# Hybrid decoder step on one core: the order of work set by a clock that follows each tile's data, attention halves ordered by events, output projection in order 0, 4, 1, 5

## The chip, the cores and the metric

The kernel runs on one core of a Trainium2 chip. The metric is the device time of one execution in microseconds (us). Three runs of the kernel before are given; their median is its time.

## The reference

One inference step of a two-layer decoder, model width 1024, for a prompt of 512 tokens and for 8 samples of 8 new tokens each, so 576 columns with the same weights. All is float32. Cut to what matters:

```python
def layer(x, ...):                         # x: tokens x 1024
    proj = rmsnorm(x, norm1) @ w_in        # 2304 for q, k, v; 512 for u; 1024 + 1024 for the gates
    q, k, v, u, ga, gb = split(proj)
    q, k = rope(q), rope(k)                # 12 heads of 64: groups (window 128, dilation 1), (512, 4), (2048, 16)
    o_a = attention(q, k, v)               # per group; the groups mixed by softmax of their log-sums
    o_b = pool(u) @ pool_lin * pool_scale  # causal means over 2, 4, 8, 16 tokens, less the token
    x = x + (sigmoid(ga) * (o_a @ w_pa) + sigmoid(gb) * (o_b @ w_pb)) @ w_o
    return x + square(relu(rmsnorm(x, norm2) @ w_up)) @ w_down
```

The samples attend to caches of 128, 512 and 1024 tokens and to their own new tokens. Updated caches and pooling states are outputs as well.

## The kernel before, in words

A float32 matrix product is made of three products: each operand is split into a high and a low part (hi, lo), and hi x hi, hi x lo and lo x hi are added up in PSUM. Weights come in tiles of 128 x 1024 through SyncE's DMA queue into `raw` (two buffers); ScalarE copies the high part (`wh`), VectorE subtracts the low part (`wl`). `wnext` (L218) hands out the next split tile, starts the reads that follow, and settles the splits that are owed.

Each layer runs these stages in TensorE's order:
- Projections to q, k, v, in units d, a, b, e, c for half 0 of the heads and d, a, b, c for half 1 (`qkv`, L535). `unit_out` (L564) scales a unit's result into `nat`, rotates it (`rope`), transposes it (`trq`), and writes it out (`out_p<-nat`). For unit c it sends the values through DRAM and back into `vc`.
- Beside them attention runs as generators. `prompt(p)` (L634) makes for half p four sets of scores (`sp`), adds the mask (`P<-sp`), reduces maxima (`stt<-P`), exponentiates, brings the sums of the groups across partitions with small matmuls (`ex<-xt`), scales P (`P<-P,cc`), transposes it (`trx`) and multiplies by the values; it ends with the event ("O", p). `decode_q` (L767) rotates the samples' queries (`rope<-dn`), sends them through DRAM (`DQ`, `DR`) and reads them spread over partitions (`qb`). `decode(p)` (L820) multiplies cached keys (`kc`) by `qb` on GpSimd (`prod`), reduces on VectorE (`SC<-prod`), makes the softmax (`dsm`, `mb`, TensorE's `po<-const,dsm`), and multiplies by cached values (`pb`).
- Pooling: four projections to u (`u<-mm,rb`), `windows` (L991), `lin` (L1038).
- Gates of the pooling branch (`tb`, `mB`), gates of the attention branch (`m`), eight blocks each.
- Output projection (L1170): eight blocks f; each result is added into `xs[f]` (`xr<-xr,mm`), and `blocks(f)` (L1146) prepares the operands of the MLP from it: a block under 4 needs one scaling, one subtraction and one split, a block of 4 or above needs six VectorE operations (it combines x[f] with x[f - 4]). `square` adds the squares for the norm.
- MLP with a Strassen-like scheme on the first product: `first_pairs` (L1281), then `both(j)` (L1307), then the end.

The instructions of all engines are written out by one pass of Python; each engine runs its own in that order. The order of the work beside TensorE's main stream is set by a small clock `now` (L240). Every step of a matrix product calls `tick` (L252), which advances `now` by a constant (0.72, 1.28, 0.85 or 0.4 us); small matmuls call `spend` (L249). `tick` then gives each waiting generator (`side`) one step if its time has come or the event that it waits for is marked (`mark`); `until` ticks until an event is there. `after(*lanes)` (L294) makes a generator wait until the queue of an engine is empty by the model of `Lane` (L276), which knows per engine a fixed cost and a rate, but not what an operation's data wait for. DMAs cost the model nothing.

## Time and profile before

| | |
|---|---|
| three runs | 1778.17, 1773.99, 1765.66 us |
| their median | 1773.99 us |
| profiled execution | 1766.39 us |
| span of its trace | 1764.6 us |
| busy: TensorE, VectorE, ScalarE, GpSimd | 1643.5, 1186.3, 667.1, 432.1 us |
| mean granted clock of TensorE | 0.959 |

The span goes from the first instruction to the last of the profiled execution; what lies around it is 1.8 us. A clock of 1.00 is the upper of TensorE's two levels (2.4 GHz); a mean of 0.9 in a stretch says that for a part of it the lower (1.2 GHz) was granted. Busy time is shown for each engine by itself; an engine that is not busy may wait for another or have nothing to do.

### The profile page before, as it was taken

How to read it: one execution, taken by the hardware profiler on the slowest of the kernel's cores; microseconds unless marked ns; L12 is line 12 of the kernel's file. 1: busy time of each engine (PE TensorE's matmuls, PEld its weight loads, DVE VectorE, ACT ScalarE, POOL GpSimd, SP SyncE). 2: the span in 40 equal slices, each digit the busy share in tenths (PEclk: the TensorE clock that was granted, in tenths of full speed). 3: DMA queues.
4: the chain of work that ended last, by engine and by line, in shares of the span. 5: the costliest groups of instructions: out<-in, count | busy, mean ns of one | idle time of the engine just before them, and what ended most of it. 6: DMA issues, size and time to landing. Idle time of an engine off the chain costs nothing. (4 is left out here: it accounts for less than half of the span.)

```text
span 1764.6 us, 30680 instructions
## 1 busy us (share of the span) xinstructions
PE 1643.5 (93%) x12608; PEld 1594.6 (90%) x12608; DVE 1186.3 (67%) x1801; ACT 667.1 (38%) x1142; POOL 432.1 (24%) x461
## 2 busy tenths in 40 slices
PE   8978798999899999999898897989997999999995
PEld 7978788989899999999898886888997999999995
DVE  6498579735776766666626985893467766666763
ACT  4523332223454434344434342321344443344443
POOL 2074129211111111121103702562111111111202
PEclk9989899999899999999999998999998999999998
DMA  4551654434235554552427346525250544554511
GB/s 172 169 180 59 211 160 125 136 104 142 105 120 191 181 169 167 189 189 70 138 74 232 116 139 189 145 90 162 76 203 29 180 169 179 191 175 165 178 63 54
DMA packets 140006, 255.21 MB, mean 145 GB/s; under 512 B 9661, under 2 KB 100285, under 8 KB 137035
## 3 DMA queue, kind: packets, MB, share of 16 engines
q1 hardware_dynamic: 135498, 198.46, 35.0%
q0 software_dynamic: 3648, 53.98, 8.5%
q8 instruction: 99, 1.62, 0.4%
q10 hardware_dynamic: 720, 0.82, 0.1%
q14 instruction: 41, 0.33, 0.1%
HBM read 239.40 MB, written 74.87 MB: 178 GB/s over the span
## 5 line engine op out<-in xcount | busy, mean ns | idle before, releaser
L316 PE MATMUL mm<-m,wh 128*128 128x256 f32 (+1 forms) x2304 | 399.6, 295 | 2.0 <-DVE xr L291 1.1
L316 PEld LDWEIGHTS mm<-m,wh 128*128 128x128 f32 x2304 | 343.9, 188 | 2.9 <-issue 1.3
L291 DVE TENSOR_TENSOR wl<-raw,wh 128x1024 fp32r<-128x1024 f32 (+2 forms) x195 | 264.6, 1358 | 105.7 <-ACT wh L291 103.2
L291 POOL TENSOR_TENSOR prod<-kc,qb 128x1024 f32<-128x1024 f32 (+1 forms) x96 | 210.3, 2222 | 221.4 <-DMA kc<-in_c 178.1
L291 ACT CAST wh<-rawu 128x512 fp32r<-128x512 f32 (+1 forms) x158 | 123.1, 783 | 352.1 <-DVE rawu L291 301.4
L316 PE MATMUL mm<-m,wl 128*128 128x256 f32 (+1 forms) x1152 | 247.1, 296 | 1.8 <-DVE wl L291 1.8
L291 ACT CAST wh<-raw 128x1024 fp32r<-128x1024 f32 (+2 forms) x195 | 183.3, 940 | 170.8 <-PE mm L316 58.7
L316 PE MATMUL mm<-a,wh 128*128 128x256 f32 (+1 forms) x1280 | 235.4, 307 | 10.6 <-DVE mB L291 5.5
L546 PE MATMUL mmq<-wh,a 128*128 128x256 f32 x1152 | 225.9, 296 | 4.4 <-DVE a L291 2.5
L316 PEld LDWEIGHTS mm<-a,wh 128*128 128x128 f32 x1280 | 196.1, 195 | 18.7 <-issue 18.1
L546 PEld LDWEIGHTS mmq<-wh,a 128*128 128x128 f32 x1152 | 188.1, 200 | 8.0 <-DVE a L291 3.2
L316 PEld LDWEIGHTS mm<-m,wl 128*128 128x128 f32 x1152 | 193.0, 188 | 2.3 <-DVE wl L291 2.3
L291 POOL COPY pace<-beat 1x1 f32<-1x1 f32 x112 | 60.7, 542 | 540.3 <-DVE beat L291 540.3
L291 DVE TENSOR_TENSOR wl<-rawu,wh 128x512 fp32r<-128x512 f32 (+1 forms) x158 | 143.8, 911 | 63.1 <-ACT wh L291 60.5
L1217 PE MATMUL pa<-h,wh 128*128 128x288 f32 x896 | 181.6, 295 | 0.0
L291 DVE TENSOR_TENSOR xr<-xr,mm 128x576 f32<-128x576 f32 (+2 forms) x152 | 108.7, 716 | 106.5 <-PE mm L316 93.1
L546 PE MATMUL mmq<-wl,a 128*128 128x256 f32 x576 | 167.9, 292 | 0.0
L1217 PEld LDWEIGHTS pa<-h,wh 128*128 128x128 f32 x896 | 144.8, 188 | 0.0
L316 PE MATMUL mm<-a,wl 128*128 128x256 f32 (+1 forms) x640 | 139.4, 300 | 0.0
L1217 PE MATMUL pa<-h,wl 128*128 128x288 f32 x448 | 132.4, 296 | 0.0
L546 PEld LDWEIGHTS mmq<-wl,a 128*128 128x128 f32 x576 | 115.1, 200 | 0.0
L316 PEld LDWEIGHTS mm<-a,wl 128*128 128x128 f32 x640 | 110.4, 194 | 0.0
(226 smaller groups left out, 2744.1 us busy)
## 6 DMA issues: line engine op xcount, KB each, us to landing
out_s<-in_c POOLq DMA_DIRECT2D x64, 508.0 KB, 5.0
rawu<-in_wup SPq DMA_DIRECT2D x60, 512.0 KB
raw<-in_wd SPq DMA_DIRECT2D x60, 512.0 KB
kc<-in_c SPq DMA_DIRECT2D x40, 512.0 KB
raw<-in_wq SPq DMA_DIRECT2D x35, 512.0 KB
kc<-in_c SPq DMA_DIRECT2D x64, 256.0 KB
out_s<-in_c POOLq DMA_DIRECT2D x32, 504.0 KB, 5.3
raw<-in_wgb SPq DMA_DIRECT2D x16, 512.0 KB
```

Source lines behind the costliest of these rows:

```text
L291: return op(*args, **kw)
L316: T.matmul(ps[:, c0:c0 + t1 - t0], w, act[:, x, t0:t1], start=(i == 0 and j == 0), stop=(i == n - 1 and j == 2))
L546: T.matmul(psm[:, j], x, ww, start=(k == 0 and i == 0 and j % 2 == 0), stop=(k == 7 and i == 2 and j % 2 == 1), skip_group_check=True)
L1217: T.matmul(dst, w[m][:, c], ops[name][k][:, x], start=(start and k == 0 and j == 0), stop=(stop and k == 3 and j == 2), skip_group_check=True)
```

## The change

No operation is added to the device's work or taken from it, but for the order. Five things change.

1. The clock. `tick()` no longer advances time, and `spend` is gone. TensorE's engine is wrapped in a class `Matrix`, and `Lane` is rewritten: each operation starts, in the model, when its engine is free and when the data that it reads (and the buffers that it writes) are ready, tile by tile, region by region (`place`, `due`, `note`). DMAs are modelled by `transfer` (270 GB/s on one wire, 1.9 us to land). VectorE's two-input operations take longer in the model while GpSimd's lane is in use. `now` is TensorE's modelled time. `ready(*aps)` is a wait for given data.
2. Halves by events. `prompt(1)` waits for ("O", 0); so does the read of `vc` for half 1, which moved into a generator `turn`; the rotation of unit d of half 1 waits for ("S", 0), the event of half 0's scores.
3. The output projection takes its blocks in the order 0, 4, 1, 5, 2, 6, 3, 7, with the weights in that order too. The squares are numbered by position.
4. `stats` waits for the squares' sum before its matmuls, and its start after the output projection is 1.0 instead of 5.0 us of the clock.
5. `both(j)` waits for the norm's event ("R", ("b", l)).

The diff, cut:

```diff
+WO = (0, 4, 1, 5, 2, 6, 3, 7)
...
-        seq += [(a["wo"][l, f], 1024) for f in range(8)]
+        seq += [(a["wo"][l, f], 1024) for f in WO]
@@ -273 @@
+    def due(outs, ins, me):
+        t = 0.0
+        for x in ins:
+            key, a = place(x)
+            t = max([t] + hits(slots[key][1], a, me))
+        for x in outs:
+            key, a = place(x)
+            t = max([t, slots[key][0]] + hits(slots[key][1], a, me) + hits(slots[key][2], a, me))
+        return t
...
             def run(*args, **kw):
-                x = kw.get("in_", kw.get("out", args[0] if args else None))
-                n = 1
-                for d in x.shape[1:]:
-                    n *= d
-                self.t = max(self.t, now[0]) + self.fixed + n / self.rate
+                outs, ins = operands(args, kw)
+                if name == "dma_start":
+                    transfer(self, outs, ins)
+                    return op(*args, **kw)
+                t = max(self.t, due(outs, ins, self))
+                d = max(size(x) for x in outs + ins) / self.rate
+                if self is V and G.t > t and sum(x.space != PSUM and size(x) > 128 for x in ins) > 1:
+                    d = min(1.4 * d, 0.7 * d + G.t - t)
+                t += self.fixed + d
...
+                self.t = t
+                note(outs, ins, t, self)
                 return op(*args, **kw)
...
+    def transfer(lane, outs, ins):
+        lane.t = max(lane.t, due(outs, ins, None)) + (0.5 if lane is G else 0.06)
+        n = 4e-3 * outs[0].shape[0] * size(outs[0])
+        wire[0] = max(wire[0], lane.t) + n / 270.0
+        note(outs, ins, wire[0] + 1.9, wire)
+
+    class Matrix:
...
+        def go(self, out, ins, cost):
+            self.t = max(self.t, due([out], ins, self)) + cost
+            now[0] = max(now[0], self.t)
+            note([out], ins, self.t, self)
+
+        def matmul(self, out, w, x, **kw):
+            n = size(x)
+            self.go(out, (w, x), n * 0.458e-3 if x.dtype == F32R else max(0.2, n * 1.7e-3))
+            return self.eng.matmul(out, w, x, **kw)
...
-    V = Lane(V, 0.07, 960.0)
-    S = Lane(S, 0.19, 1400.0)
-    G = Lane(G, 0.1, 460.0)
+    T = Matrix(T)
+    V = Lane(V, 0.13, 960.0)
+    S = Lane(S, 0.19, 1190.0)
+    G = Lane(G, 0.12, 440.0)
+    Q = Lane(Q, 0.0, 1.0)
@@ gemm @@
-            tick(0.72)
+            tick()
@@ stats @@
+        yield ready(sqs)
@@ unit_out @@
-            if unit == "c":
-                DV = drp.tile([512, 256], F32, tag=f"dv{l}{p}", name="DV")
-                vc = pp.tile([128, 4, 256], F32, tag="vc", name="vc", bufs=1)
-                vcs[p] = vc
-                post(1.2, lambda: Q.dma_start(DV.rearrange("(j p) f -> p j f", j=4), nat))
-                post(4.0, lambda: Q.dma_start(vc, DV.rearrange("(n r) f -> n r f", r=4)))
-                mark("V", unit, p, lat=9.0)
...
+            if p and unit == "d":
+                yield ("S", 0)
+            if unit == "c":
+                side(turn(p, nat))
...
+        def turn(p, nat):
+            DV = drp.tile([512, 256], F32, tag=f"dv{l}{p}", name="DV")
+            Q.dma_start(DV.rearrange("(j p) f -> p j f", j=4), nat)
+            yield 2.8
+            if p:
+                yield ("O", 0)
+            vcs[p] = pp.tile([128, 4, 256], F32, tag="vc", name="vc", bufs=1)
+            Q.dma_start(vcs[p], DV.rearrange("(n r) f -> n r f", r=4))
+            mark("V", "c", p, lat=3.0)
+
         def prompt(p):
+            if p:
+                yield ("O", 0)
             yield ("T", "b", p)
@@ output projection @@
-        for f in range(8):
-            if f == 0:
+        for i, f in enumerate(WO):
+            if i == 0:
...
-            square(xs[f], sqs, f)
-        side(stats(sqs, False, ("b", l)), 5.0)
+            square(xs[f], sqs, i)
+        side(stats(sqs, False, ("b", l)), 1.0)
@@ both @@
+            until("R", ("b", l))
```

What this does to the order of instructions is shown at three places of layer 0. First, VectorE around the small product `ex` of half 0, in the second half of the projections (`xt` is its input, `SC<-prod` the reduces of decode's products). Before:

```order
L291 TENSOR_REDUCE stt<-P 128x2 x2
L291 TENSOR_TENSOR wl<-raw,wh 128x1024
L291 TENSOR_REDUCE SC<-prod 128x8x2
L291 TENSOR_TENSOR xt<-stt,const 128x16x2 x2
L291 TENSOR_REDUCE SC<-prod 128x8x2
L291 COPY ct<-ex 128x16
L291 TENSOR_TENSOR cc<-ct,stt 128x8
```

and now:

```order
L352 TENSOR_TENSOR wl<-raw,wh 128x1024
L352 SCALAR_TENSOR_TENSOR dn<-psd,rs,dt 64x128
L352 SCALAR_TENSOR_TENSOR ve_257<-psd,rs,dt 64x128
L352 TENSOR_REDUCE SC<-prod 128x8x2 x2
L352 TENSOR_TENSOR xt<-stt,const 128x16x2 x2
L352 TENSOR_REDUCE SC<-prod 128x4x2
L352 TENSOR_TENSOR wl<-raw,wh 128x1024
L352 TENSOR_REDUCE SC<-prod 128x4x2
L352 TENSOR_REDUCE SC<-prod 128x8x2 x2
L352 SCALAR_TENSOR_TENSOR dn<-psd,rs,dt 64x256
L352 TENSOR_TENSOR wl<-raw,wh 128x1024
L352 COPY ct<-ex 128x16
```

Two reduces stand ahead of `xt` instead of one. What follows `ct` (the sums, and behind them the scalings and transposes of P) stands later too, behind more of the reduces. The rotation of decode's queries (`rope<-dn`) stands one weight split later than before. On SyncE's queue the read `qb<-DR` now stands in front of a weight read (`raw<-in_wq`) that stood before it, and two reads of `kc` follow.

Second, TensorE where the projections end and the pooling projections (`mm<-a`) begin: the scores of half 1 (`sp`), set by set. Before (six matmuls `mm` are one step of the clock, eight steps one projection):

```order
L316 MATMUL mm<-a,wl 128x256
L316 MATMUL mm<-a,wl 128x320
L654 MATMUL sp<-Td 128x256 x2
L657 MATMUL sp<-Tb,Ta 128x128 x4
L316 MATMUL mm<-a,wh 128x256
L316 MATMUL mm<-a,wh 128x320
L316 MATMUL mm<-a,wh 128x256
L316 MATMUL mm<-a,wh 128x320
L316 MATMUL mm<-a,wl 128x256
L316 MATMUL mm<-a,wl 128x320
L883 MATMUL po<-const,mb 128x16
L316 MATMUL mm<-a,wh 128x256
```

and now:

```order
L375 MATMUL mm<-a,wl 128x256
L375 MATMUL mm<-a,wl 128x320
L375 MATMUL sp<-Td 128x256 x2
L375 MATMUL sp<-Tb,Ta 128x128 x4
L379 MATMUL po<-const,mb 128x16
L375 MATMUL sp<-Td 128x256 x2
L375 MATMUL sp<-Tb,Ta 128x128 x4
L375 MATMUL sp<-Td 128x256 x2
L375 MATMUL sp<-Tb,Ta 128x128 x4
L375 MATMUL po<-dsm,const 128x16
```

Before, the last two of the four sets stand apart by projections, and the first two stand in the last unit. Now all four stand behind that unit, three of them without a projection between.

Third, VectorE in the first gates, at the softmax of decode of half 1 (`dsm`; `mt` and `mb` follow TensorE's `po<-const,dsm`). Before:

```order
L291 TENSOR_TENSOR wl<-raw,wh 128x512
L291 TENSOR_TENSOR SC<-SC,const 128x368
L291 TENSOR_REDUCE dsm<-SC 128x16
L291 TENSOR_REDUCE mt<-po 16x8
L291 COPY mb<-mt 16x128
L291 TENSOR_TENSOR tb<-mm,rb 128x576
L291 TENSOR_TENSOR SC<-SC,po 128x368
L291 TENSOR_TENSOR wl<-raw,wh 128x1024
L291 TENSOR_REDUCE dsm<-SC 128x16
```

and now:

```order
L352 TENSOR_TENSOR wl<-raw,wh 128x512
L352 TENSOR_TENSOR SC<-SC,const 128x368
L352 TENSOR_REDUCE dsm<-SC 128x16
L352 SCALAR_TENSOR_TENSOR mB<-tb,mm 128x576
L352 TENSOR_TENSOR wl<-raw,wh 128x1024
L352 TENSOR_REDUCE mt<-po 16x8
L352 COPY mb<-mt 16x128
L352 TENSOR_TENSOR SC<-SC,po 128x368
L352 TENSOR_TENSOR tb<-mm,rb 128x576
L352 TENSOR_REDUCE dsm<-SC 128x16
```

The chain from `dsm` on stands earlier, and an `mB` and a whole weight split lie within it. On TensorE `po<-const,dsm` stands 102 matmuls (17 steps of six) earlier.

In the output projection VectorE's operations are the same, block by block, in the new order of blocks.

## Rows read from the trace of the kernel before

**Rows 1.** The page's first part: span, and busy time of each engine.
```profile
span 1764.6 us, 30680 instructions
...
PE 1643.5 (93%) x12608; PEld 1594.6 (90%) x12608; DVE 1186.3 (67%) x1801; ACT 667.1 (38%) x1142; POOL 432.1 (24%) x461
```

**Rows 2.** Busy time by stage, six of layer 0, two of layer 1.
```profile
core 0: us, PE busy (x) PEld busy (x) DVE busy (x) ACT busy (x) POOL busy (x), PEclk, DMA share, GB/s
84.15:183.03 98.88, 83.78 (x649) 79.56 (x647) 84.97 (x107) 31.23 (x59) 51.71 (x24) 0.90 0.45 135
183.03:212.72 29.69, 19.14 (x139) 17.52 (x139) 15.45 (x26) 11.24 (x37) 5.93 (x12) 0.84 0.81 261
248.00:332.70 84.70, 78.50 (x574) 76.49 (x572) 80.87 (x83) 22.54 (x37) 53.29 (x24) 0.98 0.36 106
332.70:372.00 39.30, 36.90 (x335) 32.20 (x334) 13.20 (x24) 6.72 (x11) 10.78 (x19) 0.91 0.58 170
372.00:429.00 57.00, 57.00 (x430) 57.00 (x428) 28.28 (x36) 19.52 (x28) 8.82 (x7) 1.00 0.29 91
429.00:506.00 77.00, 67.79 (x471) 66.97 (x470) 53.62 (x83) 37.59 (x62) 9.22 (x7) 0.89 0.36 120
950.10:1047.93 97.83, 82.97 (x649) 79.25 (x648) 84.73 (x107) 31.26 (x59) 50.74 (x24) 0.91 0.44 135
1112.00:1200.00 88.00, 79.51 (x580) 77.29 (x578) 77.76 (x86) 23.17 (x38) 54.55 (x24) 0.98 0.37 109
```

**Rows 3.** TensorE's timeline: start us, us, instruction, [idle before, what ended it].
```profile
94.02 1.22 PE L686 MATMUL ex<-xt,const 128*128 128x16 f32 x5 [3.95 <-DVE xt L291]
...
117.44 0.30 PE L733 MATMUL trx<-const,P 128*128 128x128 f32 x1 [1.85 <-DVE P L291]
...
156.41 0.88 PE L609 MATMUL trq<-const,nat 128*128 128x128 f32 x3 [4.01 <-DVE nat L291]
...
207.93 0.80 PE L905 MATMUL po<-pb,kvn 128*128 128x128 f32 x2 [9.11 <-POOL pb L291]
...
480.39 0.82 PE L1217 MATMUL mm<-h,wh 128*128 128x288 f32 x2 [6.18 <-DVE xr L291]
```

**Rows 4.** VectorE's operations by form, 84 to 160 us: count, busy, mean ns.
```profile
L291 DVE TENSOR_SCALAR P<-P,cc 128x256 f32<-128x256 f32 x14 | 17.3, 1277 | 0.0
L291 DVE TENSOR_TENSOR wl<-raw,wh 128x1024 fp32r<-128x1024 f32 x6 | 11.5, 1913 | 0.9 <-ACT wh L291 0.9
```

**Rows 5.** The same view, 208 to 248 us.
```profile
L291 DVE TENSOR_SCALAR P<-P,cc 128x256 f32<-128x256 f32 x14 | 4.3, 349 | 0.0
```

**Rows 6.** Timelines of GpSimd and VectorE at decode's first products.
```profile
87.87 9.60 POOL L291 TENSOR_TENSOR prod<-kc,qb 128x1024 f32<-128x1024 f32 x5 [70.88 <-DMA kc<-in_c]
...
90.34 1.22 DVE L291 TENSOR_REDUCE SC<-prod 128x16 f32<-128x1024 f32 x1 [3.55 <-POOL prod L291]
91.47 2.40 DVE L291 TENSOR_TENSOR xt<-stt,const 128x32 f32<-128x32 f32 x2
```

**Rows 7.** Timelines of VectorE and of SyncE's queue: the way of decode's queries.
```profile
63.46 0.61 DVE L291 TENSOR_TENSOR rope<-dn,const 64x192 f32<-64x192 f32 x2
...
66.71 1.23 DVE L291 TENSOR_TENSOR wl<-raw,wh 128x1024 fp32r<-128x1024 f32 x1 [2.18 <-ACT wh L291]
...
77.48 0.33 SPq L780 DMA_DIRECT2D qb<-DR  x1
```

**Rows 8.** VectorE's timeline, a set of scores and the first pooling projection.
```profile
191.91 1.29 DVE L291 TENSOR_TENSOR P<-sp,const 128x512 f32<-128x512 f32 x2 [0.30 <-PE sp L657]
193.11 1.27 DVE L291 TENSOR_REDUCE stt<-P 128x2 f32<-128x512 f32 x2
...
205.30 0.69 DVE L291 TENSOR_TENSOR u<-mm,rb 128x512 f32<-128x512 f32 x1 [10.22 <-DMA out_p<-nat]
```

**Rows 9.** VectorE's timeline: the adds of output blocks 6 and 7.
```profile
469.55 0.75 DVE L291 TENSOR_TENSOR xr<-xr,mm 128x576 f32<-128x576 f32 x1
...
479.49 0.75 DVE L291 TENSOR_TENSOR xr<-xr,mm 128x576 f32<-128x576 f32 x1
```

More of the change, by code (lines that the diff above doesn't have):

```diff
@@ L247, in mark @@
         ev[key] = now[0] + lat
-    def spend(us):
-        now[0] += us
     def tick(us=0.0):
@@ L274, in until, with place @@
             assert n < 2000, key
+    slots, seen, count = {}, {}, {}
+    def place(x):
+        t = x.tensor
+        key = seen.get(t.name)
+        if key is None:
+            k = (t.slot_key, t.tag) if getattr(t, "slot_key", None) is not None else (t.name, None)
+            n = count[k] = count.get(k, -1) + 1
+            key = seen[t.name] = (k, n % (getattr(t, "bufs", None) or 1))
+            old = slots.get(key)
+            slots[key] = [max([old[0]] + [e[4] for e in old[1] + old[2]]) if old else 0.0, [], []]
+        (step, n), *rest = x.ap
+        p0, lo = divmod(x.offset, step) if step else (0, x.offset)
+        return key, (p0, p0 + n, lo, lo + sum((c - 1) * abs(d) for d, c in rest) + 1)
@@ new lines, in is_ap, with hits @@
+    def is_ap(x):
+        return hasattr(x, "ap") and hasattr(x, "tensor")
+    def hits(es, a, me):
+        return [e[4] + (0.0 if e[5] is me else 0.1) for e in es
+                if e[0] < a[1] and a[0] < e[1] and e[2] < a[3] and a[2] < e[3]]
+    def due(outs, ins, me):
[7 more added lines that the diff above has]
+        return t
@@ new lines, in note, with operands @@
+    def note(outs, ins, end, me):
+        for xs_, w in ((outs, 1), (ins, 2)):
+            for x in xs_:
+                key, a = place(x)
+                es = slots[key][w]
+                es[:] = [e for e in es if not (a[0] <= e[0] and e[1] <= a[1] and a[2] <= e[2] and e[3] <= a[3]
+                                               and e[4] <= end)][-60:]
+                es.append((*a, end, me))
+    def operands(args, kw):
+        aps = [x for x in args if is_ap(x)]
+        outs = [kw["out"]] if "out" in kw else [aps.pop(0)]
+        if kw.get("accum_out") is not None:
+            outs.append(kw["accum_out"])
+        return outs, aps + [v for k, v in kw.items() if k not in ("out", "accum_out") and is_ap(v)]
@@ L276, in hybrid_decoder_kernel, with size @@
+    def size(x):
+        n = 1
+        for d in x.shape[1:]:
+            n *= d
+        return n
     class Lane:
         def __init__(self, eng, fixed, rate):
-            self.eng, self.fixed, self.rate, self.t = eng, fixed, rate, 0.0
+            self.eng, self.fixed, self.rate, self.t, self.table = eng, fixed, rate, 0.0, None
         def __getattr__(self, name):
             op = getattr(self.eng, name)
-            if name == "dma_start":
-                return op
             def run(*args, **kw):
-                x = kw.get("in_", kw.get("out", args[0] if args else None))
-                n = 1
-                for d in x.shape[1:]:
-                    n *= d
-                self.t = max(self.t, now[0]) + self.fixed + n / self.rate
+                outs, ins = operands(args, kw)
[7 more added lines that the diff above has]
+                t += self.fixed + d
+                f = args[2] if name == "activation" else None
+                if f in (AF.Exp, AF.Sqrt, AF.Tanh) and f != self.table:
+                    self.table = f
+                    t += 1.3
+                self.t = t
+                note(outs, ins, t, self)
@@ L291, in run, with __init__, transpose @@
                 return op(*args, **kw)
             return run
+    wire = [0.0]
+    def transfer(lane, outs, ins):
[4 more added lines that the diff above has]
+    class Matrix:
+        def __init__(self, eng):
+            self.eng, self.t = eng, 0.0
+        def go(self, out, ins, cost):
[6 more added lines that the diff above has]
+            return self.eng.matmul(out, w, x, **kw)
+        def transpose(self, out, x, one):
+            self.go(out, (x, one), 0.108)
+            return self.eng.transpose(out, x, one)
@@ L294, in after, with ready @@
     def after(*lanes, lag=0.2):
         return "at", max([now[0]] + [x.t for x in lanes]) + lag
-    V = Lane(V, 0.07, 960.0)
-    S = Lane(S, 0.19, 1400.0)
-    G = Lane(G, 0.1, 460.0)
+    def ready(*aps, lag=0.2):
+        return "at", max(now[0], due([], aps, None)) + lag
+    T = Matrix(T)
[3 more added lines that the diff above has]
+    Q = Lane(Q, 0.0, 1.0)
     def post(delay, fn):
@@ L335, in pair8 @@
                                  start=(k == 0 and j == 0), stop=(k == 7 and j == 2))
-                tick(0.72)
+                tick()
         return [ps[:, 256:832] for ps in tiles]
@@ L940, in decode @@
                         if s % 4 == 3:
-                            spend(0.4)
                             yield 0.1
@@ L1169, in hybrid_decoder_kernel @@
         sqs = tp.tile([128, NT], F32, tag="sqs", name="sqs", bufs=1)
-        for f in range(8):
-            if f == 0:
+        for i, f in enumerate(WO):
+            if i == 0:
                 first = pair8(mixed)
-            elif f == 1:
+            elif i == 1:
                 wnext()
-            ps = first.pop(0) if f < 2 else gemm8(wnext(), mixed)
+            ps = first.pop(0) if i < 2 else gemm8(wnext(), mixed)
             V.tensor_add(xs[f], xs[f], ps)
             blocks(f)
-            square(xs[f], sqs, f)
-        side(stats(sqs, False, ("b", l)), 5.0)
+            square(xs[f], sqs, i)
+        side(stats(sqs, False, ("b", l)), 1.0)
         mark("ffn", l, lat=8.0)
@@ L1218, in product @@
                              stop=(stop and k == 3 and j == 2), skip_group_check=True)
-                tick(0.4)
+                tick()
         def relu2(z, f):
```

21 lines of the change are left out of this document (3 added, 18 removed).

## The prediction

> **What bounds the kernel now.** I read the page's first part first: TensorE is busy for 1643.5 of 1764.6 us, VectorE for 67%, the others for less [rows 1]. So the program is TensorE's own work, plus the time in which it waits, plus the time in which it works at half clock. Then I cut the span into the stages of the program and read busy time and granted clock of each [rows 2]. From 372 to 429 us (output projection) TensorE is busy for all 57.00 us at clock 1.00: nothing is to be had there. The losses lie in five stages of each layer. Those of layer 0, as idle time and as (1 - clock) times length:
> A, the second half of the projections (84.15 to 183.03): 98.88 - 83.78 = 15.1 idle, up to 9.9 of clock. Part of the clock's loss is idle time itself, so I count 8.4 of it: 23.5.
> S, from projections to pooling (183.03 to 212.72): 10.6 idle, up to 4.7 of clock: 14.
> B, the first gates (248 to 332.7): 6.2 idle, 1.7 of clock: 8.
> C, the end of decode attention (332.7 to 372): 2.4 idle, 3.5 of clock: 6.
> D, end of the output projection and start of the MLP (429 to 506): 9.2 idle, up to 8.5 of clock: 14.
> Layer 1 shows the same in A (97.83 - 82.97 = 14.9 idle, clock 0.91) and 8.5 idle in B (88.00 - 79.51). Together some 66 us a layer, 132 in all. The larger gaps, and what ended each, are the third view [rows 3]: in A results of VectorE (xt at 94.02, P at 117.44, nat at 156.41), in S GpSimd's pb, in D VectorE's add into xr.
>
> **Why TensorE waits in A.** VectorE is busy for 84.97 of the 98.88 us there, which is more than TensorE needs for its own work [rows 2]. A large part of this is not work: the 14 scalings of P of 256 columns take 1277 ns each while GpSimd runs its products [rows 4], and 349 ns in the other half, where it runs few [rows 5]. That is 0.93 us each, 13 us in all. The weight splits (wl), which have two inputs in SBUF as well, take 1913 ns there, and 1.23 us at 66.71, before the products begin [rows 4, 7].
>
> The Trainium skill gives a rule for this (SBUF — State Buffer, Who interferes with whom): VectorE and GpSimd arbitrate for one port pair by an exclusive lock, and the loser is fully blocked for the whole instruction of the other. Rows 4, 5 and 7 agree: the slow forms lose less than the time of one product (1.92) each. The rule speaks against a part of the change: GpSimd's products are the same in number, so whatever two-input operation is moved into their time is blocked as P was. Were every scaling's place taken by such an operation, the saving of part 1 on VectorE would be nothing and the time below 1732 + 2 x 10.5 = 1753, inside the range.
>
> **Part 1: half 0's softmax and P V are spread out.** The planner's new model knows VectorE's queue, so the scalings and transposes of P, which stood between the third and fifth unit, now lie one or two units later; in VectorE's order twelve of the sixteen stand behind nearly all reduces of the products. I take 12 x 0.93 = 11 us off VectorE: 84.97 - 11 = 74, where TensorE at full clock needs 83.78 - 8.4 = 75. So the waits for P and nat and the small ones between them (some 10 us of the 15.1) go.
> The first wait does not go. At 90.34 VectorE waits 3.55 us for GpSimd's first product, and xt stands behind that reduce; so TensorE waits 3.95 us at 94.02 [rows 3, 6]. In the new order two such reduces stand ahead of xt. The product may come later too: the rotation of the decode queries (63.46) now stands behind the next weight split, which ended at 67.94, and the reads that bring qb (issued 77.48, the product began at 87.87) hang on it [rows 6, 7]. So the first product starts at 87.87 + 4.5 = 92.4, two of them end (9.60 / 5 = 1.92 each) at 96.2, then a reduce of 1.22 and two xt of 2.40 together: 99.8. TensorE comes to this place 32 matmuls later than before, 83.78 / 649 = 0.13 us each, so at 94.02 - 3.95 + 4.1 = 94.2. New wait: some 6 us. Behind it on TensorE are projections, which nothing else waits for. Bounds: 0 (qb is now issued ahead of a weight read, which makes the 4.5 us good) and 12 (that weight read lands late, and the split in front of xt waits for it). With 2 us of small waits and 5 of clock, A costs 13 instead of 23.5: -10.5.
>
> **Part 2: the halves by events.** Half 1's attention now waits for the output of half 0, so its four sets of scores, two of which stood in the last unit, all lie in the first pooling projections; three of them stand without a projection between them. Each needs two adds of 1.29 us together, and leaves VectorE two reduces of 1.27 [rows 8]. VectorE needs 2.6 us a set, TensorE's six matmuls at 0.14 (78.50 / 574) 0.8, so it waits up to 1.7 us a set, 5 us for the three, and 0.5 for the sum behind them. In return the 9.11 us at 207.93 go: there VectorE waited 10.22 us (to 205.30) for the writes of the last unit's keys and values, whose space the pooling buffers take [rows 3, 8], and GpSimd's pb stood behind that. In the new order these writes are issued at the same place of SyncE's queue, but the score sets fill the time. With 1.5 of clock S costs 7 instead of 14: -7. Bounds: 0 (the writes land last again, behind the scores) and -11.
>
> **Part 3: decode of half 1 comes sooner.** TensorE's first instruction of its softmax (po from dsm) stands 17 steps of six matmuls earlier in the gates, 17 x 6 x 78.50 / 574 = 14 us [rows 2]. VectorE cannot follow: in B it is busy for 80.87 of 84.70 us. What now stands behind dsm on it are two mB, one tb, two half and one whole weight split, some 5 us. So it needs 76, where TensorE without waits comes after 84.7 - 6.2 - 14 = 64.5: B waits some 11 to 12 us instead of 6.2, with clock 14 to 15 instead of 8: +7. Bounds: 0 (the late operations of the gates cover the dsm chain as they did) and +14 (all of the 14 us returns as a wait). In C the rest of this decode now lies among the gates and is over before its buffer is wanted; I take 5 of the 6: -5.
>
> **Part 4: output projection in order 0, 4, 1, 5.** The wait of 6.18 us at 480.39 is for the add of the last block into xr [rows 3]. VectorE goes from one block of the upper four to the next in 479.49 - 469.55 = 9.9 us [rows 9], against TensorE's 48 x 57.00 / 430 = 6.4 [rows 2]. The order permutes VectorE's chain and leaves its sum: the last is block 7 in both, and its add starts when all the rest is done. Nor does it save the start of the MLP, since block 3 is now the last but one. Sums of squares read a step later hide small waits: -1.3. Bounds: -14 (all of D: light blocks between heavy ones let VectorE keep up) and +5 (half of the 9.9 us, if block 3's operand, made behind block 7's start in that chain, becomes the last thing that the MLP waits for).
>
> **The rest.** The new clock and the wrappers issue nothing. TensorE's and VectorE's instructions are the same in number. The other stages keep their order but for a few places. The sums of squares that end layer 0 are read 3.4 us of work later, which hides up to that; I take 2.
>
> **Sum.** Layer 0: -10.5 - 7 + 7 - 5 - 1.3 = -17. Layer 1: the same with B only +5 (its idle time was 8.5) and 2 at its start: -21. Together -38. From the profiled execution's 1766.39 us that is 1728. That execution was one of the lower of its kind (the three runs have a median of 1773.99), so I expect the median of the changed kernel a few us above the sum: **1732 us**.
>
> **Rivals.**
> 1. All that waits is moved out of the way: the product is there when xt is wanted, VectorE keeps up in B, and D shrinks by half. Then A 5, S 4, B 7, C 1, D 7: 24 of 66 remain, 2 x 42 = 84 less: 1683. For it: TensorE has slack elsewhere in each of these stages. Against it: VectorE's 80.87 of 84.70 in B. Chance 0.15.
> 2. The waits only change place: A gives 4, S 3, C 5, D 1, and B takes back 9, so 4 a layer: 1758 by the sum, 1762 by the median. For it: VectorE's work is the same but for the collisions, and these can fall on other operations. Chance 0.22.
> 3. Slower, by the decode queries. TensorE's place for xt is tied to GpSimd's first product, which starts 87.87 - 63.46 = 24.4 us after the rotation [rows 6, 7]. Each us by which it starts later than I have it (4.5 after now) is a us more of TensorE's wait, in both layers, and the split of the next weights stands behind the reduces, so nothing else can run. The gain of 38 is used up when the product comes 4.5 + 19 = 24 us later than now, that is when the way from rotation to product takes about twice as long. At two and a half times (4.5 + 37 = 41 later) the time is 1774 + 2 x 18 = 1810. For it: the reduces of the products stand in front of xt, two instead of one. Against it: the queries' reads stand earlier in SyncE's queue, not later. Chance 0.07.
> That the clock doesn't do what it says is no case of its own: the order differs on every engine.
>
> The forecast has 0.56, the rivals 0.15, 0.22 and 0.07. The forecast's own range is 1708 to 1754; with rival 2 whole and most of the way to rival 1 the range is **1690 to 1768**. A measurement of this kernel tells about 1% from no change: under 1756 is faster, over 1792 slower. Faster: nearly all of the forecast (0.54), rival 1 (0.15) and little of rival 2 (0.03): 0.72. Slower: rival 3 but for its part below 24 us, and some for a mishap of its size in B: 0.07. Same: the rest, 0.21.
>
> **What would show it.** Right: in A no wait of TensorE for P or nat, and one of some 6 us for xt; scalings of P near 350 ns in both halves; in S no wait for pb, but three of 1 to 2 us at the scores; in B more idle time than 6.2, ended by mB, tb or dsm; in C next to none; in D still a wait for xr of 3 to 6 us. Wrong: no wait at xt, or idle time in B under 5 (then rival 1); scalings still over 1 us; VectorE's wait for the writes of out_p still there (then rival 2); a first product after 112 us (then rival 3).

## The result, and the profile after

The changed kernel takes 1783.75 us (median of 11 runs, 1779.14 to 1788.09); the kernel before takes 1768.37 beside it (11 runs). The ratio is 1.0079, 95% interval 1.006 to 1.0099. So it is slower by 14 us, where 1732 was forecast. The profiled execution has a span of 1781.3 us.

The page's first part of the kernel after:

```profile
span 1781.3 us, 30681 instructions
...
PE 1650.3 (93%) x12608; PEld 1598.0 (90%) x12608; DVE 1179.5 (66%) x1801; ACT 668.1 (38%) x1142; POOL 429.0 (24%) x461
```

Against [rows 1] the span grew by 16.7 us. TensorE's idle time went from 1764.6 - 1643.5 = 121.1 to 131.0, 9.9 more, and its busy time grew by 6.8 with the same 12608 matmuls: more of them ran at half clock (mean granted clock 0.958 against 0.959).

Busy time by stage of the kernel after, cut near the same places of the program as [rows 2] (columns as there; the third row is the stretch between S and B):

```profile
core 0: us, PE busy (x) PEld busy (x) DVE busy (x) ACT busy (x) POOL busy (x), PEclk, DMA share, GB/s
83.87:180.88 97.01, 78.08 (x602) 75.71 (x600) 80.05 (x97) 25.87 (x41) 52.72 (x24) 0.88 0.50 155
180.88:207.87 26.99, 24.19 (x183) 21.52 (x181) 17.07 (x33) 14.91 (x45) 4.83 (x9) 0.87 0.76 238
207.87:250.96 43.09, 39.81 (x397) 32.88 (x396) 30.28 (x65) 11.39 (x24) 10.78 (x16) 0.96 0.49 141
250.96:336.00 85.04, 72.77 (x512) 70.82 (x512) 73.33 (x85) 20.21 (x33) 48.37 (x24) 0.94 0.43 124
336.00:376.00 40.00, 40.00 (x369) 34.23 (x368) 11.49 (x19) 6.90 (x11) 8.56 (x18) 1.00 0.42 128
376.00:433.00 57.00, 57.00 (x430) 57.00 (x429) 28.27 (x36) 19.50 (x28) 9.02 (x7) 1.00 0.29 91
433.00:517.00 84.00, 67.45 (x472) 65.94 (x471) 53.91 (x83) 37.90 (x62) 9.23 (x7) 0.94 0.35 119
```

Idle time in A is 18.9 us (15.1 before), in S 2.8 (10.6), in B 12.3 (6.2), in C none (2.4), in D 16.6 (9.2). Instructions have moved across these cuts, so the stages up to the gates are also read as one stretch, from 60 us to the place from which both kernels run the attention gates without a wait (372 us before, 376 after). The kernel before:

```profile
60.00:372.00 312.00, 277.74 (x2253) 257.72 (x2252) 233.73 (x330) 95.23 (x197) 126.94 (x89) 0.93 0.50 152
```

and after:

```profile
60.00:376.00 316.00, 278.60 (x2257) 257.57 (x2256) 228.20 (x330) 95.85 (x198) 125.26 (x89) 0.93 0.50 150
```

The same work takes 4.0 us more, 3.1 of it idle time. In D it takes 84.00 - 77.00 = 7.0 more. These two make up layer 0's loss.

The whole difference can be read from single matmuls. At the first matmul of layer 0's output projection the kernel after is 3.9 us behind (423.60 against 419.67). At layer 1's first projection it is 11.2 us behind (887.00 against 875.80), and 72 matmuls of the projections later only 6.4 (898.32 against 891.91): some 5 us come back where layer 1 opens. At the first matmul of layer 1's output projection it is 9.1 us behind (1295.82 against 1286.73), at the end of the span 16.7. So in both layers the larger loss lies behind the first matmul of the output projection.

The larger waits of TensorE in layer 0 of the kernel after ([rows 3] before), and its first instruction on `dsm` of half 1:

```profile
100.11 1.86 PE L375 MATMUL ex<-xt,const 128*128 128x16 f32 x8 [5.50 <-DVE xt L352]
129.99 0.58 PE L375 MATMUL psd<-wh,hd 128*128 128x256 f32 x1 [9.31 <-DVE dn L352]
...
197.58 1.08 PE L375 MATMUL sp<-Td 64*128 64x256 f32 x3 [1.09 <-DVE P L352]
...
247.29 0.58 PE L375 MATMUL lp<-pa,wlh 128*128 128x256 f32 x1 [3.28 <-DVE pa L352]
260.78 1.03 PE L379 MATMUL trp<-const,u 128*15 128x128 f32 x4 [3.99 <-DVE ob L352]
...
282.26 0.87 PE L375 MATMUL mm<-ob,wh 128*128 128x256 f32 x2 [1.92 <-DVE ob L352]
...
287.22 1.33 PE L375 MATMUL mm<-ob,wh 128*128 128x256 f32 x4 [3.82 <-DVE tb L352]
...
326.51 0.27 PE L379 MATMUL po<-const,dsm 128*16 128x128 f32 x1
...
447.75 0.53 PE L375 MATMUL mm<-m,wl 128*128 128x256 f32 x2 [4.26 <-DVE wl L352]
487.76 0.50 PE L375 MATMUL mm<-h,wh 128*128 128x288 f32 x2 [3.37 <-DVE xr L352]
...
504.99 0.82 PE L375 MATMUL mm<-h,wh 128*128 128x288 f32 x2 [5.45 <-DVE z L352]
```

The waits for P, nat and pb of [rows 3] are gone. In their place stand one of 9.31 us for `dn`, one of 2.82 (at 163.17) for ScalarE's `PT`, those for the pooling operands `pa` and `ob`, and one in the middle of the output projection.

The wait of 9.31 us, followed back on VectorE and GpSimd:

```profile
111.01 3.52 DVE L352 TENSOR_REDUCE SC<-prod 128x16 f32<-128x1024 f32 x4
114.45 7.49 DVE L352 TENSOR_TENSOR wl<-raw,wh 128x1024 fp32r<-128x1024 f32 x1
121.86 1.21 DVE L352 TENSOR_REDUCE SC<-prod 128x16 f32<-128x1024 f32 x1
...
129.47 0.47 DVE L352 SCALAR_TENSOR_TENSOR dn<-psd,rs,dt 64x256 f32<-64x256 f32 x1
...
112.29 8.56 POOL L352 TENSOR_TENSOR prod<-kc,qb 128x512 f32<-128x512 f32 x4 [1.31 <-DVE SC L352]
```

A weight split that takes 1.23 us alone [rows 7] took 7.49: it began within a run of four products on GpSimd, beside the second, and ended after the last of them (112.29 + 8.56 = 120.85). So it was held through three products. `dn`, which frees the PSUM tile that TensorE wants, stands behind it. By form, VectorE in A after (columns as in [rows 4]):

```profile
L352 DVE TENSOR_TENSOR wl<-raw,wh 128x1024 fp32r<-128x1024 f32 x10 | 19.1, 1909 | 5.5 <-ACT wh L352 5.5
L352 DVE TENSOR_TENSOR rope<-nat,const 128x256 f32<-128x256 f32 x6 | 9.3, 1593 | 0.0
L352 DVE TENSOR_SCALAR P<-P,cc 128x256 f32<-128x256 f32 x14 | 6.5, 503 | 0.0
```

The scalings of P fell from 1277 to 503 ns (350 were forecast). But the rotations now take 1593 ns each. To count all of it I took for each form of VectorE's instructions the shortest duration in any trace of this study, and summed what each row of the timeline takes over that (rows with over 0.15 us). This lost time in A is 33.0 us before (P 16.1, wl 4.2, rotations 1.1) and 31.7 after (P 3.4, wl 7.0, rotations 7.1). About 6 us of either count come of the counting and are no loss: a row joins reduces of 1.21 and of 0.67 us. What is left, 27 and 26 us, changed its place and kept its size.

### The profile page after: what moved, and what is told of

Same layout as the page of the kernel before. It is cut to its first block, busy times and chain, and to the rows that moved or that the text cites. A ratio compares the mean times of both kernels' runs of the same rounds, so it can differ in the third digit from the quotient of the medians.

```text
span 1781.3 us, 30681 instructions
## 1 busy us (share of the span) xinstructions
PE 1650.3 (93%) x12608; PEld 1598.0 (90%) x12608; DVE 1179.5 (66%) x1801; ACT 668.1 (38%) x1142; POOL 429.0 (24%) x461
## 4 chain that ended last, share of the span: by engine, by line
PE 70%; DVE 13%; ACT 5%; issue 5%; DMA 3%; POOL 2%; SPq 1%; POOLq 0%; DVEq 0%; ACTq 0%
PE mm L375 37%; PE pa L375 10%; PE mmq L375 7%; PE pc L375 5%; DVE wl L352 4%; PE pb L375 2%; POOL prod L352 2%; PE po L375 2%; DVE SC L352 2%; ACT wh L352 2%; PE psd L375 1%; DMA kc<-in_c 1%; DVE cc L352 1%; DVE xr L352 1%; PE O L375 1%
## 5 line engine op out<-in xcount | busy, mean ns | idle before, releaser
L375 PE MATMUL mm<-m,wh 128*128 128x256 f32 (+1 forms) x2560 | 450.8, 297 | 4.7 <-DVE xr L352 3.3
L375 PEld LDWEIGHTS mm<-m,wh 128*128 128x128 f32 x2560 | 386.6, 189 | 6.1 <-issue 2.5
L352 DVE TENSOR_TENSOR wl<-raw,wh 128x1024 fp32r<-128x1024 f32 (+2 forms) x195 | 246.0, 1262 | 69.0 <-ACT wh L352 66.1
L375 PE MATMUL mm<-m,wl 128*128 128x320 f32 (+1 forms) x1280 | 281.5, 297 | 10.2 <-DVE wl L352 10.2
L375 PEld LDWEIGHTS mm<-m,wl 128*128 128x128 f32 x1280 | 217.5, 189 | 11.1 <-DVE wl L352 11.1
L352 DVE TENSOR_REDUCE SC<-prod 128x16 f32<-128x1024 f32 (+1 forms) x96 | 96.4, 1030 | 25.5 <-POOL prod L352 25.3
```

Source lines behind the costliest of these rows:

```text
L352: return op(*args, **kw)
L375: return self.eng.matmul(out, w, x, **kw)
```

## The experiments

Every ratio is against runs of the kernel before on the same chip. On a time of 1770 us, 0.001 is 1.8 us.

**The output projection: e1, e2, e3, e9.** VectorE in the kernel after, where the second block (block 4) is added:

```profile
439.99 0.75 DVE L352 TENSOR_TENSOR xr<-xr,mm 128x576 f32<-128x576 f32 x1 [3.23 <-DMA xr<-in_x]
...
445.26 3.56 DVE L352 TENSOR_TENSOR wl<-raw,wh 128x1024 fp32r<-128x1024 f32 x2
```

VectorE waits 3.23 us for block 4's part of x, which is read fifth. Block 4's six operations and the two weight splits follow, and TensorE stops at 447.75 for the second split. So four runs took the order of blocks and the order of reading x apart.

e1, the changed kernel with the old order of blocks:

```diff
-WO = (0, 4, 1, 5, 2, 6, 3, 7)
+WO = tuple(range(8))
```

> The changed kernel with the output projection in order 0 to 7 again; all else of the change stays. Theory 1 (block 4 comes second, but its part of x is the fifth to be read, so VectorE's add waits 3.23 us for it and the weight splits behind it come late): both the wait of 4.26 us for a split at 447.75 and the longer start of the MLP go, about 7 us a layer, 14 in all: 1783.75 - 14 = 1770. Theory 2 (the loss in this stretch comes from the new clock and the earlier sum of squares, not from the order of blocks): within 3 us of 1783.75.

Measured: 1775.20 us, ratio 1.0032 (1.0014 to 1.005), 8 us under the changed kernel, where 14 were expected. The wait for wl is gone; the 6.18 us for xr are back.

e2, the kernel before with the new order of blocks alone:

```diff
-        for f in range(8):
+        for i, f in enumerate(WO):
...
```

> The kernel before with the output projection in order 0, 4, 1, 5, 2, 6, 3, 7 alone (weights, blocks and squares by position). Theory 1: slower by 10 to 14 us: 1768 + 12 = 1780, with a wait of TensorE for wl of about 4 us some 14 us into the output projection of each layer. Theory 2: within 3 us of 1768, no such wait.

Measured: 1781.38 us, ratio 1.0059 (1.0038 to 1.008): 10 us more. TensorE's waits in e2:

```profile
444.69 0.85 PE L317 MATMUL mm<-m,wl 128*128 128x256 f32 x2 [4.26 <-DVE wl L292]
```

The same wait of 4.26 us appears under the old clock: it belongs to the order of blocks.

e3, the changed kernel with x read in that order:

```diff
-            post(2.1 + 0.8 * k, lambda k=k: Q.dma_start(xs[k], ...))
+            post(2.1 + 0.8 * WO.index(k), lambda k=k: Q.dma_start(xs[k], ...))
```

> The changed kernel with the reads of x into xs issued in the order of the blocks (0, 4, 1, 5, ...). Theory 1: VectorE's wait for xr<-in_x (3.23 us) and TensorE's wait for wl (4.26) go in both layers; VectorE's chain up to block 7 is the limit behind it, so of 7 us a layer 3 to 6 come back: 1772 to 1778. Rival (block 4 is heavy and stands in front of two splits, whatever its data): the wait for wl stays at 3 us or more, 1782 to 1785.

Measured: 1775.89 us, ratio 1.0027 (1.0008 to 1.0046), 9 us under the changed kernel, as much as the old order gives. VectorE and TensorE in e3:

```profile
438.89 0.76 DVE L352 TENSOR_TENSOR xr<-xr,mm 128x576 f32<-128x576 f32 x1
...
444.17 3.59 DVE L352 TENSOR_TENSOR wl<-raw,wh 128x1024 fp32r<-128x1024 f32 x2
...
446.68 0.53 PE L375 MATMUL mm<-m,wl 128*128 128x256 f32 x2 [1.19 <-DVE wl L352]
```

The add of block 4 no longer waits, and of 4.26 us of TensorE's wait 1.19 are left.

e9, both edits in the kernel before:

> The kernel before with the new order of output blocks and x read in the order of the blocks. Theory 1 (the order loses by x alone): what the order alone costs there (about 10 us) falls to 0 to 3: 1770 to 1773, and the wait for wl of 4.26 us is under 1.5. Rival (block 4 early is too heavy for VectorE by itself): 1778 or more.

Measured: 1769.43 us, ratio 1.0011 (0.9996 to 1.0026). The mechanism of theory 1 is borne out by all four runs, though e1 gave less than its 14 us: the order of blocks costs 8 to 10 us of the 14, by x being read in another order than it is used; with x in order it costs nothing that can be told, and gains nothing either. Some 5 us of the 14 remain in e1 and e3, and no run here takes them apart.

**The wait for dn: e4.** The changed kernel, with the request for the sum ahead of a unit's weights:

```diff
+            if (p, unit) != (0, "d"):
+                until("psd")
+                del ev[("psd",)]
...
             psm = mmp.tile([128, 4, 256], F32, tag="mm", name="mmq")
```

> The changed kernel in which each projection unit asks for the sum dn of the unit before (which frees the PSUM tile psd) at its start instead of at its half, so dn is issued ahead of the weight splits of that unit. Theory A (TensorE's wait of 9.31 us at 129.99 is for dn, which stands on VectorE behind a weight split that GpSimd's products hold up for 7.49 us): the wait falls under 3 us in both layers, 10 to 14 us less: 1770 to 1774. Rival (VectorE's load is what counts): the wait moves to a weight split or to xt, the time stays within 4 us of 1783.75.

Measured: 1784.31 us, ratio 1.0087 (1.0061 to 1.0114), no gain. TensorE's larger waits in A:

```profile
98.14 0.58 PE L375 MATMUL mmq<-wl,a 128*128 128x256 f32 x1 [6.65 <-DVE wl L352]
...
123.92 1.88 PE L375 MATMUL ex<-xt,const 128*128 128x8 f32 x8 [3.84 <-DVE xt L352]
...
152.59 0.58 PE L375 MATMUL psd<-wh,hd 128*128 128x256 f32 x1 [6.24 <-DVE dn L352]
```

The wait moved to a weight split, to xt and to a later dn; VectorE's lost time in A is 32.6 us, counted in the same way. The rival holds: to move this one operation ahead in VectorE's queue gained nothing.

**The products beside VectorE: e5, e6.** One row of each key product is multiplied and the rest filled, in the kernel before and in the changed one, with the order of all other instructions as it was:

```diff
+    op(pr[:, 0:1], kk[:, 0:1], q[:, 0:1])
+    return eng.memset(pr[:, 1:], 0.0)
```

> The kernel before, in which GpSimd multiplies one of the 4 or 8 rows of each of decode's key products and fills the others with zeros (a fill reads nothing from SBUF); this leaves out most of the products' work, the order of every other instruction stays. Theory A (VectorE's time lost beside GpSimd's products is what TensorE waits for in stages A and B): VectorE loses under 8 us in A where it loses 31.6 now, scalings of P take about 350 ns, and the waits for P, nat and mB fall: 25 to 35 us less, 1735 to 1745. Rival (VectorE's own work and its order bound A and B): within 10 us of 1769.

> The changed kernel with the same edit (one row of each key product multiplied, the rest filled; this work is left out). Theory A: the wait of 9.31 us for dn and those of 3.28 and 3.99 us in the pooling stage fall under 2 us; 40 to 55 us less, 1730 to 1744, so that against the kernel before with the same edit only the loss of the output projection is left: -5 to +5 us, where the whole change costs 14. Rival (the new order itself is worse in A to C): it stays 10 us or more behind the kernel before with the same edit.

Measured: 1703.59 us for the kernel before, ratio 0.9622 (0.9598 to 0.9647), and 1710.93 for the changed one, 0.9665 (0.9636 to 0.9693). Both are shorter by more than expected, 66 and 73 us: that much does the left-out work cost each order. VectorE's lost time in A falls to 12.5 and 7.3 us (some 6 of either are the reduces of the counting). P's scalings in e5 take 730 ns, not 350. The wait for dn and that for pa are gone; 2.58 us of the one for ob stay. The edit does two things that these runs do not separate: VectorE is held less, and GpSimd has its results sooner (it is busy for 340.8 us in e5 and 432.1 before). The difference between the two kernels is 7 us, between the forecasts of the theory (-5 to +5) and of the rival (10 or more). From 60 us to the last projection of the gates, e5:

```profile
60.00:345.00 285.00, 271.95 (x2308) 254.91 (x2307) 197.46 (x335) 97.94 (x201) 81.89 (x138) 0.97 0.56 169
```

and e6, with the same matmuls:

```profile
60.00:349.00 289.00, 277.03 (x2308) 257.43 (x2308) 190.48 (x333) 97.79 (x201) 79.64 (x138) 0.97 0.54 166
```

Idle time is 13.1 and 12.0 us: nothing is gained there even without the products. But e6 is 5.1 us longer in busy time. Most of e5's idle time lies in two waits side by side (7.53 and 1.45 us), that of e6 in four places (2.81, 1.09, 2.58 and 2.19 us). The granted clock (third number from the right) in the one long stretch at half clock that e5 has there:

```profile
179.24:192.89 13.65, 6.97 (x29) 6.71 (x30) 7.11 (x19) 1.41 (x3) 6.94 (x14) 0.50 0.51 173
```

and in the four of e6:

```profile
140.59:144.00 3.41, 3.37 (x16) 3.37 (x17) 3.38 (x7) 1.09 (x1) 0.00 (x0) 0.50 0.46 144
178.14:184.97 6.83, 6.13 (x27) 5.95 (x26) 5.41 (x11) 5.57 (x20) 2.96 (x7) 0.50 0.57 193
232.75:236.16 3.41, 2.68 (x12) 2.49 (x13) 1.93 (x4) 1.61 (x4) 2.71 (x5) 0.50 0.07 18
256.64:260.05 3.41, 3.41 (x17) 3.41 (x16) 3.41 (x5) 0.06 (x1) 2.16 (x4) 0.50 0.50 164
```

TensorE works for 7.0 us at half clock in e5, where the waits themselves fill half of the stretch, and for 15.6 in e6. That accounts for most of the 5.1 us in these two executions; that of e6 is 3.5 us above its median. It is no rule that separate waits cost more: in D of the changed kernel the waits of 3.37 and 2.31 us lie in a stretch at full clock,

```profile
484.00:500.00 16.00, 8.70 (x63) 7.76 (x62) 11.29 (x20) 8.51 (x16) 0.23 (x1) 1.00 0.03 8
```

and D has more idle time than before at a higher clock (16.6 us at 0.94, 9.2 at 0.89). The wait of 4.01 us for wl in the output projection is still in e6 and adds to the difference. So the products are a burden of about the same size on both orders, and do not explain the difference between them.

**Smaller parts: e7, e8, e13, e11.** e7, e3's kernel with the norm's sums placed as before:

```diff
-        yield ready(sqs)
-        side(stats(sqs, False, ("b", l)), 1.0)
+        side(stats(sqs, False, ("b", l)), 5.0)
```

> The changed kernel with x read in the order of the blocks, and with the norm's sums placed as before (a start 5.0 of the clock after the output projection, no wait for the squares). Theory: the waits at the start of the MLP (2.31, 1.02 and 4.06 us for z) come from these sums, and go back towards 1.23 and 1.80: 4 to 8 us less than with x alone (1775.9): 1768 to 1772. Rival (they come from the order of blocks, with heavy block 7 and light block 3 last): within 2 us of 1775.9.

Measured: 1773.65 us, ratio 1.0034 (1.0012 to 1.0056), which can't be told from e3 (1.0027). At the start of the MLP the waits for z (2.31, 1.02, 4.06 us) became 2.68 for the squares and 1.98 for z. Not settled.

e8, e3's kernel with half 1's products held back:

```diff
             yield (6.0, 0.5)[p]
+            if p:
+                yield ("pg", 0, l)
```

It is aimed at the pooling stage of the changed kernel, on VectorE and GpSimd:

```profile
240.68 3.07 DVE L352 SCALAR_TENSOR_TENSOR pg<-s,u 128x512 f32<-128x512 f32 x2
243.68 2.89 DVE L352 TENSOR_TENSOR wll<-wr,wlh 128x512 fp32r<-128x512 f32 x1
...
240.93 5.08 POOL L352 TENSOR_TENSOR prod<-kc,qb 128x1024 f32<-128x1024 f32 x2 [12.26 <-DMA kc<-in_c]
```

and in the kernel before:

```profile
244.78 0.83 DVE L291 SCALAR_TENSOR_TENSOR pg<-s,u 128x512 f32<-128x512 f32 x2
245.53 0.69 DVE L291 TENSOR_TENSOR wll<-wr,wlh 128x512 fp32r<-128x512 f32 x1
...
248.19 5.48 POOL L291 TENSOR_TENSOR prod<-kc,qb 128x1024 f32<-128x1024 f32 x2 [10.75 <-DMA kc<-in_c]
```

The first products of half 1 now stand beside pg and wll, for which TensorE waits; before they began 2 us after them.

> The changed kernel with x read in the order of the blocks, and half 1's key products held back until the last pooling operand pg is computed. Theory A: the two waits of TensorE in the pooling stage (3.28 for pa, 2.86 to 3.99 for ob) go, since pg, wll and pa no longer stand beside products: 8 to 14 us less than 1775.9, if decode of half 1 still ends in time: 1762 to 1768. Rival: the products then collide with the weight splits of the gates and the waits move to stage B or to the end of decode: 1773 to 1780.

Measured: 1776.74 us, ratio 1.0046 (1.0028 to 1.0065), no gain against e3. TensorE still waits 3.10 and 2.77 us for pa, and in the gates 2.13 for wl, 1.99 and 2.56 for tb. But the edit did not do what it was for. In e8's trace GpSimd and VectorE still meet:

```profile
235.40 4.81 POOL L352 TENSOR_TENSOR prod<-kc,qb 128x1024 f32<-128x1024 f32 x2 [11.62 <-DMA kc<-in_c]
...
237.90 3.00 DVE L352 SCALAR_TENSOR_TENSOR pg<-s,u 128x512 f32<-128x512 f32 x2
240.82 0.68 DVE L352 TENSOR_TENSOR wll<-wr,wlh 128x512 fp32r<-128x512 f32 x1
```

The products were written out later, but GpSimd's own queue reached them as soon as `kc` had landed, before VectorE reached this pg. Of the operations named, only wll and the last pg (0.83 us at 249.41) are clear of products. The time lies in the rival's range, but theory A was not tested.

e13, the events of the change in the kernel before, without the new clock:

```diff
+            if p and unit == "d":
+                yield ("S", 0)
...
+            if p:
+                yield ("O", 0)
```

> The kernel before, its clock as it was, with the events of the change alone: half 1's attention waits for the output of half 0, and the rotation of unit d of half 1 for half 0's scores. Theory (the new clock, not the events, moves the waits of stages A to C; under the old clock the events shift two rotations, one set of transposes and little else): within 3 us of 1768. Rival (the events carry the loss of 3 to 4 us a layer in A to C): 1774 to 1777.

Measured: 1767.52 us, ratio 0.9977 (0.9954 to 0.9999). The events cost nothing under the old clock, so the loss in A to C comes with the new clock, alone or together with the events. The new clock without the events was not tried: half 1's scores would then wait for the one buffer of P while its last reads by half 0 stand behind them. How large that loss is, one trace does not say: the traces of e10 and e14, which are the same kernel, differ by 4 us at the end of this stretch.

e11, the kernel before with the sums that open layer 1 later:

```diff
-            side(stats(sqs, True, ("a", l + 1)), 2.4)
+            side(stats(sqs, True, ("a", l + 1)), 6.0)
```

> The kernel before with the matmuls on the sums of squares that open layer 1 half a unit later (a start of 6.0 instead of 2.4 of the clock), as the changed kernel has them. Theory: the 4 to 5 us that the changed kernel gains at this seam come from it: 3 to 5 us less, 1765 to 1767. Rival (the gain comes from elsewhere): within 1.5 us of 1770.

Measured: 1764.67 us, ratio 0.9983 (0.9964 to 1.0002). The wait of 2.08 us for the squares is gone in the trace; the gain of some 3 us in the whole time is not told from none. The place itself, between layer 0's MLP and layer 1's projections, is shorter by 4.5 us in e11's trace and by 4.8 in the changed kernel's.

**A scaling less on VectorE: e10, e12, e14, e15.** The scalings of P on ScalarE, which is busy for 31.23 of 98.88 us in A [rows 2]:

```diff
...
-                V.tensor_scalar(out=pj[:, 256:], in0=pj[:, 256:], scalar1=cc[:, 2, j, hh:hh + 1], ...)
+                S.activation(pj[:, 256:], pj[:, 256:], AF.Copy, scale=cc[:, 2, j, hh:hh + 1])
```

In the kernel before, e10:

> The kernel before with the scalings of P on ScalarE (32 activations a half instead of 32 scalings on VectorE's queue in 16 places; the same values). Theory A in the form that collisions cost where VectorE has an operation with two SBUF inputs or a scaling beside a product: P's 16 us of lost time in A go and are not taken over, the waits for P and nat fall, 8 to 16 us less: 1754 to 1762. Rival (whatever VectorE has next is held up instead, so that the lost time in A stays near 30 us): within 4 us of 1770.

Measured: 1753.08 us, ratio 0.9919 (0.9894 to 0.9945): 14 us less. On ScalarE the 14 scalings of 256 columns take 501 ns each:

```profile
L291 ACT ACTIVATE P<-P,cc 128x256 f32<-128x256 f32 x14 | 6.4, 501 | 0.0
```

VectorE's lost time in A falls to 18.4 us, and the waits for P are gone; two for nat stay (1.11 and 3.29 us). In the changed kernel, e12:

> The changed kernel with the scalings of P on ScalarE. Theory A: few scalings of P stand beside products here (3.4 us lost in A), so little is gained: within 4 us of 1783.75. Rival (ScalarE's load or VectorE's own work counts): 5 us or more to either side.

Measured: 1787.67 us, ratio 1.0115 (1.01 to 1.013), 4 us more than without the edit, and 6 by the ratios to the kernel before on each chip, which is outside what theory A gave. The lost time is 28.2 us there. Where few of the scalings stand beside the products, moving them gains nothing; why it costs was not followed up.

e14 is e10's kernel once more, and e15 adds the edit of e11 to it.

> The kernel before with the scalings of P on ScalarE once more, as one look beside the next run: 1748 to 1756.

> The kernel before with the scalings of P on ScalarE and the sums that open layer 1 half a unit later. Theory (the two gains lie in different stages and add): 14 + 2.7 = 17 us less, 1749 to 1753. Rival (the second gain is hidden by the first or was none): 1753 to 1757.

Measured: 1757.29 us in one execution of e14, beside runs of the kernel before with a median of 1771.73; and for e15 1758.06, ratio 0.9916 (0.9893 to 0.9939). Both lie 1 us above their ranges, on a chip where the kernel before takes 4 us more than on e10's. e15 can't be told from e10. In its trace the start of layer 1 is 4.4 us shorter all the same, so a second gain of that size is lost elsewhere or in the scatter. Either version is some 14 us under the kernel before.

## Why the prediction was wrong

- **What bounds the kernel** was read rightly: TensorE's waits and half clock are the whole difference (9.9 and 6.8 us).
- **Part 1 is the first step that failed.** The instructions went where it said: the waits for P and nat are gone, P's scalings are short, the first product came at 90.20 (92.4 forecast), and TensorE waits 5.50 us for xt (6 forecast). What failed is "I take 12 x 0.93 = 11 us off VectorE". The lost time stayed (33.0 and 31.7 us, counted as above), since rotations and weight splits took P's place beside the products, and the 15.1 us of idle time became 18.9 instead of 8. The Trainium skill's rule (SBUF — State Buffer, Who interferes with whom), weighed there as speaking against the change, was the better guide to this step. It has the loser wait for one instruction of the other; here one split waited through three. e5 and e6 bear out that products are what VectorE loses its time to, and e10 that it is saved by taking the operation off VectorE. The prediction also read [rows 4] too smoothly. The mean of 1913 ns of the weight splits is five of 1.21 to 1.43 us and one of 5.20, beside five products in a row:

```profile
148.89 5.20 DVE L291 TENSOR_TENSOR wl<-raw,wh 128x1024 fp32r<-128x1024 f32 x1 [0.95 <-ACT wh L291]
...
142.31 10.69 POOL L291 TENSOR_TENSOR prod<-kc,qb 128x1024 f32<-128x1024 f32 x5 [1.36 <-DVE SC L291]
```

So "less than the time of one product (1.92) each" holds for the mean alone: what one split can lose, 4 us, stood in the trace of before.
- **Part 2** held at its own place: no wait for pb, short ones at the scores (0.62 and 1.09 us where three of up to 1.7 were forecast) and 0.73 for decode's dsm behind them, S 2.8 us idle. What was late next stood one stage further: pa and ob, 3.28 and 3.99 us, behind pg and wll that now stand beside half 1's first products. I priced decode's earlier start in the gates alone.
- **Part 3** has its number by luck: 12.3 us idle in B (11 to 12 forecast). The forecast wait was TensorE's for `dsm` of half 1, and that wait did not come: `po` from `dsm` ran at 326.51 without one. Of B's idle time 5.9 us are for `ob` (3.99 and 1.92), which is part 2's collision in the pooling stage, and 6.3 for `tb` (3.82, 1.54 and 0.91), about B's 6.2 of before. C held: no idle time there.
- Parts 1 to 3 together were to give 15.5 us in layer 0; the stretch became 4.0 longer. Rival 2 (the waits only change place) describes it, but its 4 us a layer to the good did not come either.
- **Part 4 is the second step that failed**, and the larger one for the sign: -1.3 forecast, +7.0 measured in layer 0's D. "The order permutes VectorE's chain and leaves its sum" was worked out from VectorE's and TensorE's queues alone. The add's other input, x, comes by SyncE's queue in the order 0 to 7, and I didn't look when block 4's part lands. The bound of +5 was of another mechanism. e9 shows that the order costs nothing that can be told once x comes in the order of use, which is what the step had said of it. Also, [rows 2] from 372 to 429 us, which the prediction calls the output projection, is the attention gates for the most part: the output projection's first matmul stands at 419.67, and its loss falls into D.
- **The rest**, 2 us at the start of layer 1, came and was larger: 4.8 us in the trace.
- The chances: slower by over 1% did not happen, nor did faster; within 1% had 0.21. None of the rivals on the slow side was the one that came.

## What to carry to other kernels

Before counting a collision between two engines as saved, ask which operation takes its place beside the other engine's work: three orders of the same operations lost 32 to 33 us in one stage, while moving one form to a third engine with room took 14 us off the kernel before. In the changed kernel, where few of that form stood beside the products, the same move gained nothing. When a loop's order is changed, change the order of every transfer that feeds it, and read from the trace when each input lands, not only the weights. An engine that works off its own queue is not held back by a later place in the order of writing (e8): read from the trace whether an edit has moved what it was to move.

## What the runs showed of the hardware

- A VectorE operation on two SBUF inputs was held not for one GpSimd product but through three in a row, of some 2.5 us each (7.49 us against 1.23 alone); it ended when GpSimd had run out of products that it could start: the next began 2.29 us after the run, behind a wait.
- The products' price was above what the waits in the trace name: with them thinned out both kernels are 66 and 73 us shorter, while the idle time of TensorE that stood in A and B of both layers of the kernel before was some 45 us [rows 2]. In the profiled executions of the kernel before and e5, TensorE's idle time falls from 121.1 to 82.1 us and its busy time, with the same matmuls, from 1643.5 to 1621.0: the second part is half clock (mean granted clock 0.959 and 0.973).
